# A conformer block with dilated attention on one core: the far statistics' read behind the next head's loads, and one filler step behind the last gate pair

## The chip, the core and the metric

The kernel runs on 1 core of one Trainium2 chip. The metric is the device time of one execution in microseconds, as the median of several runs; before the change it is 1699.01 us (three runs, 1698.5 to 1700.75 us).

## What is computed

One layer on 1024 tokens with 1024 channels, in float32. The attention is the part that the change touches:

```
z = rms_norm(x) @ w_in            # GLU input, q, k, v, gate logits
a = silu(rms_norm(causal_conv31(a_val * sigmoid(a_gate))));  y_a = a @ w_conv_out
for window, dilation in ((128, 1), (512, 4), (2048, 16)):
    o_g, lse_g = dilated_window_attention(q, k, v, slopes, window, dilation)
o = sum_g softmax_g(lse_g) * o_g;                            y_b = o @ w_attn_out
x = x + (sigmoid(g_a) * y_a + sigmoid(g_b) * y_b) @ w_out
x = x + (silu(u_gate) * u_val) @ w_down,  u = causal_conv3(rms_norm(x) @ w_up)
```

There are 16 heads of 64 dimensions. The three groups share one softmax over their logarithms of sums, so the kernel may weigh all keys of a query in one sum.

## The kernel before, in words

Every product of float32 matrices is made of three products of rounded parts (high x high, high x low, low x high; the halves are made by `split`, ScalarE the high part and VectorE the low one). The stages follow one another on PE: projections and GLU (to 180 us), q, k and v (to 457 us), the gate logits, five pairs of gate rows by a scheme of seven half-size products (to 579 us), then attention to 874 us, the output projections, and the feed-forward part to the end.

**Gate pairs.** The loop over `PAIRS` keeps a pair's sums in a PSUM tile `gx` (X and, for early pairs, a second half) and a bank `gy` (Y). The last pair, number 4, ends with three products of twelve matmuls each: X with `b12`, Y with `b22`, X with `form["t4"]`. ScalarE then copies X out (`c21`, L880). Scores of attention take tiles of the same pool `psA` of two tiles, so a score can need the tile that this copy frees.

**Attention.** The loop over `slots` has 8 slots for each head: places 0 to 3 score the first half of the queries, place 4 scores the far keys (distance of 512 and more in steps of 4, `score_far`), places 5 to 7 the second half. In each slot the code writes, in this order: the scores; filler steps of the side gemms (`fill(front)`; a step is three 128x512 matmuls of a gate or conv-out gemm, which keep PE at work while VectorE and ScalarE make powers); the transposes of the powers of a slot 12 earlier (`flip`) and the products with v of the slot before (`weigh`); the comparison and combination of statistics; the powers; statistics' transfers; `fill(behind)`. The engines ScalarE, VectorE, PE and GpSimd keep the written order inside this block. PE may still interleave two such blocks, here the gate pairs' block and attention's. SP, which issues nearly all transfers, is ordered by the framework's scheduler: an instruction is placed when the scheduler's model holds it ready. `tc.issue_after(x)` makes the instructions inside it follow `x` on the same engine, as an order and not as a wait.

**Statistics of a head.** A query of the second half has its near keys in one layout and its far keys in another (partition = position within a residue). Each has a minimum and a sum, in the tile `own` (near `own[:, 0]`, far `own[:, 1]`). Both layouts need the other's values in the tile `other`:

- `far_out` (L992): SP writes the far statistics to DRAM (`dstat`, 4 KB), two slots after the far scores.
- `near_to_far` (L989): four transfers of 1 KB move the near statistics from partition to partition into `other[:, 1]`, one slot after place 7.
- `far_to_near` (L995): SP reads `dstat` back in the other layout into `other[:, 0]`, in code five slots (`READ`) after the far scores, that is at place 1 of the next head. It must wait until the write has landed.
- `compare` (L999, L1000) on VectorE, nine slots after the far scores, needs all five transfers. `combine` (L1005 to L1008 and GpSimd's L975) comes one slot later and scales the powers.

**Loads.** At place 1 of head h the code calls `head(h + 1)`: q (512 KB, L155), two loads of k (512 KB each, L155), the mask (320 KB, L749), into tiles with two buffers. `values` loads v and vf (L155); `stage` loads weights for the side gemms (L93); `result` stores a head's half (L1072). SP's transfers use eight semaphores in turn, so that each also waits for the landing of the one eight before it.

Of the kernel before, what the change touches and what calls it, by code (L numbers as in the profile page):

```python
# [61 lines left out]
def block_kernel(ctx: ExitStack, tc: tile.TileContext, x, xT, x0, g2, pack, mask,  # L62
                 w_first, w_ch, w_qkv, w_co, w_ao, w_o, w_up, w_down, out):
    nc = tc.nc
    act, dve, pool, pe, sp = nc.scalar, nc.vector, nc.gpsimd, nc.tensor, nc.sync
# [240 lines left out]
    if True:  # L306
# [426 lines left out]
        def conv_result(c):  # L733
# [4 lines left out]
                           scale=pk[:, C_CG + c : C_CG + c + 1])  # L738
            act.dma_start(da[:, c, :], ordered)

        def head(h):
            hp, r, g8 = h // 2, (h % 2) * DH, h // 8
            q = p2.tile([P, T], F32R, tag="q", bufs=2, name=f"q_{h}")
            kk = p2.tile([P, 2, T], F32R, tag="kk", bufs=2, name=f"kk_{h}")
            m = p2.tile([P, 640], F32, tag="m", bufs=2, name=f"m_{h}")
            fetch(q, dq[g8].rearrange("p s c t -> (p s) c t")[2 * r : 2 * r + P, hp % 4, :])
            for s in range(2):
                fetch(kk[s:P:2], dk[g8][r : r + DH, :, hp % 4, :])
            sp.dma_start(m, mask[h])  # L749
            return q, kk[:, 0], kk[:, 1], m  # L750

        cover(COVER)
# [65 lines left out]
        with tc.manual_schedule(engines=hand):  # L818
            for n in range(2):
                xz[n] = gate_first(n, firsts[n])  # L820
                begun(n)
            load(1, 0)
            for n, (a, b) in enumerate(PAIRS):
                X = xz[n][:, 0:512]
                Y = bank_ps(f"gy_{n}")
                (sh, sl), (gh, gl) = pw[n]["s12"], pw[n]["s3"]
                inner = 0 < n < N - 1
                if n + 2 < N:
                    load(n + 2, 0)
                if n == 3:  # L830
                    p1_cm.__exit__(None, None, None)
                    p2_cm = tc.tile_pool(name="ph2", bufs=1, reuse_waits="tile")
                    p2 = p2_cm.__enter__()
                    pool2.append(p2)
                if n + 1 < N:
                    load(n + 1, 1)
                if n == 3:
                    tiles[0] = head(0)
                parts(n, "s4", "s4")
                if n == 0:  # L840
                    fourth()
                if inner:
                    parts(n + 1, 0, "v")
                product(X, sh[:, 4:8], sl[:, 4:8], *form["t2"], False)
                c12 = quarter(f"c12_{n}")
                act.activation(c12, X, AF.Copy)
                product(Y, sh[:, 0:4], sl[:, 0:4], *form["t1"], True)
                p5 = quarter(f"p5_{n}")
                act.activation(p5, Y, AF.Copy)
                if n == N - 1:  # L850
                    act.activation(warm, mhalf[:, 0:7], AF.Exp)
                if n == 0:
                    rs8 = conv_factors()
                if n == 2:
                    for c in (2, 3, 4, 5):
                        conv_result(c)
                product(X, gh[:, 0:4], gl[:, 0:4], *b12, False)
                if n == 1:
                    conv_spread(rs8)
                tt_(p5, X, p5, add)  # L860
                sp.dma_start(dgate[b][:, 512:1024], p5)
                if n + 1 < N:
                    sums(n + 1)
                if inner:
                    xz[n + 1] = big_ps(f"gx_{n + 1}")
                    for i in range(2):
                        product(xz[n + 1][:, i * 512 : i * 512 + 512], *(t[:, 4 * i : 4 * i + 4] for t in pw[n + 1]["v"]),
                                *left[i], True)
                    parts(n + 1, 2, "s12")
                    begun(n + 1)  # L870
                    for c in {1: (0, 1), 2: (6, 7)}.get(n, ()):
                        conv_result(c)
                else:
                    product(Y, *pw[n]["s4"], *b22, False)
                    tt_(c12, Y, c12, add)
                    if n + 1 < N:
                        parts(n + 1, 2, "s12")
                product(X, gh[:, 4:8], gl[:, 4:8], *form["t4"], False)
                c21 = quarter(f"c21_{n}")
                act.activation(c21, X, AF.Copy)  # L880
                sp.dma_start(dgate[b][:, 0:512], c21)
                if inner:
                    product(Y, *pw[n]["s4"], *b22, False)
                if n + 1 < N:
                    parts(n + 1, 1, "s3")
                if inner:
                    tt_(c12, Y, c12, add)
                sp.dma_start(dgate[a][:, 512:1024], c12)
# [7 lines left out]
    if True:  # L896
# [89 lines left out]

        def near_to_far(h):
            for i in range(4):
                sp.dma_start(other[h][32 * i : 32 * i + 32, 1], own[h][:, 0, i])  # L989

        def far_out(h):
            sp.dma_start(dstat[h % 2], own[h][:, 1])  # L992

        def far_to_near(h):
            sp.dma_start(other[h][:, 0], dstat[h % 2].rearrange("(i a) r s -> (a r) i s", i=4))  # L995

        def compare(h):
            f = ready2("both", [P, 2, 4], F32, 2, f"both_{h}")
# [75 lines left out]
        def fill(n):  # L1074
            for _ in range(n):
                next(gates, None)
# [33 lines left out]
        with tc.manual_schedule(engines={ENG.Activation, ENG.DVE, ENG.PE, ENG.Pool}):  # L1110
# [3 lines left out]
            for at in range(len(slots) + BACK + 1):  # L1114
                count[2] += 1
                cur = slots[at] if at < len(slots) else None
                front, behind = (FRONT[at % 8], BEHIND[at % 8] + (START[at] if at < BACK else 0)) if cur else TAIL
                new = []
                if cur is not None:
                    h, half, n = cur  # L1120
                    place = at % 8
                    if place == 4:
                        statistics(h)
                    if place == 5:
                        values(h)
                    if place == 1 and h + 1 < H:
                        tiles[h + 1] = head(h + 1)
                    new = score(h, tiles[h], SCORES[half][n])
                for unit in late:
                    share(*unit)  # L1130
                if len(pieces) > 2 and apart(at):
                    piece_high(2)
                fill(front)
                for n, soon in enumerate(COPIES):
                    if at == 0 and soon < 0 or cur is not None and (at - soon) % 8 == 0 and at - soon < len(slots):
                        by_residue((at - soon) // 8 if at else 0, n)
                flips = []
                if BACK <= at < len(slots) + BACK:
                    fh, fhalf, fn = slots[at - BACK]
                    if FLIPS[fhalf][fn]:  # L1140
                        flips.append(flip(fh, fhalf, FLIPS[fhalf][fn]))
                for w in pend:
                    done = weigh(*w) or done
                pend = flips
                late = []
                if done is not None:
                    result(*done)
                    done = None
                for ago, ready in ((BACK - 2, combine), (BACK - 3, compare)):
                    if 0 <= at - ago < len(slots) and slots[at - ago][1:] == (1, 0):  # L1150
                        ready(slots[at - ago][0])
                for unit in new:
                    powers(*unit)
                if cur is not None and half == 0:
                    late = new
                for ago, n0, send in ((2, 0, far_out), (1, 3, near_to_far), (READ, 0, far_to_near)):
                    if 0 <= at - ago < len(slots) and slots[at - ago][1:] == (1, n0):
                        send(slots[at - ago][0])
                if at == len(slots):
                    p2_cm.__exit__(None, None, None)  # L1160
                    hb2.append(ctx.enter_context(tc.tile_pool(name="hb2a", bufs=1, reuse_waits="tile")))
                    oT = [[hb2[0].tile([P, KT, 512], F32R, tag=f"hb{a}0", name=f"oT{a}0")] for a in range(2)]
                    heads = [o_fetch(0, k) for k in range(0, KT - 2, 2)]
                if at - len(slots) in (4, 5, 8, 9, 10, 11, 12):
                    o_step(heads)
                if at == len(slots) + BACK - 4:
                    heads.append(o_fetch(0, KT - 2))
                if apart(at):
                    piece_low()
                fill(behind)  # L1170
                if apart(at + 1):
                    piece_high(2)
            for _ in gates:
# [627 lines left out]
```

## Time and profile before

| | |
|---|---|
| median of 3 runs | 1699.01 us (1698.5 to 1700.75) |
| the profiled execution's own time | 1695.4 us |
| its span (first to last instruction) | 1693.6 us |
| granted TensorE clock | 1.0 over the whole span |
| busy PE, VectorE, ScalarE, GpSimd | 99%, 77%, 47%, 13% of the span |
| transfers, mean over the span | 177 GB/s |
| one head in the attention stage | some 17.5 us |

The profile is of one execution. Its page sums the busy time of each engine; the views used below are the table of waits (who waited for whom: total us, times, longest us), an engine's instructions in order of time (start, duration, engine, line, operation, tiles, and in brackets the idle time ahead and what ended it), the landing times of a line's transfers, and the row of digits that gives the busy tenths of the transfer engines in 40 slices. PE is a matmul, SPq an instruction of SP's queue. Heads are counted from 0; a head's row is told by its time.

### The profile page before, as it was taken

What the parts mean: (1) busy time and instruction counts of PE and PEld (TensorE: products, weight loads), DVE (VectorE), ACT (ScalarE), POOL (GpSimd) and SP (SyncE); (2) the same over time, 40 slices, a digit from 0 to 9 for tenths busy, and PEclk for the clock granted to TensorE, in tenths of its full rate; (3) what the DMA queues carried; (4) which work ended last, traced back from release to release, by engine and by line L of the source; (5) the groups of instructions that cost most, each with busy time, mean ns of one, the idle gap of its engine ahead of it and who ended that gap; (6) DMA issues with size and microseconds to landing.
All of it is one profiled execution on the core that took longest, in us unless ns stands there. A gap on an engine that the chain in (4) does not pass through costs nothing.

```text
span 1693.6 us, 22622 instructions
## 1 busy us (share of the span) xinstructions
PE 1681.4 (99%) x7939; PEld 1397.1 (82%) x7939; DVE 1303.1 (77%) x2114; ACT 787.9 (47%) x1351; POOL 224.3 (13%) x300
## 2 busy tenths in 40 slices
PE   9999999999999999999999999999999999999999
PEld 7888888888888888888888888888888888888887
DVE  6999999999876567767658654887777677789863
ACT  5411233233245478767646433544544455543431
POOL 0000132033000255555410000000000000000000
PEclk9999999999999999999999999999999999999999
DMA  9411145344555977886769594622222222499851
GB/s 375 153 50 50 50 137 162 125 137 137 175 178 195 320 226 238 261 243 201 221 214 333 187 335 147 227 99 76 75 90 85 87 75 87 145 366 322 287 172 50
DMA packets 187121, 300.24 MB, mean 177 GB/s; under 512 B 32256, under 2 KB 90240, under 8 KB 186496
## 3 DMA queue, kind: packets, MB, share of 16 engines
q1 hardware_dynamic: 185712, 294.48, 52.1%
q10 hardware_dynamic: 1296, 4.33, 0.6%
q8 instruction: 62, 1.02, 0.2%
q14 instruction: 51, 0.42, 0.1%
HBM read 214.74 MB, written 83.95 MB: 176 GB/s over the span
## 4 chain that ended last, share of the span: by engine, by line
PE 92%; DMA 3%; DVE 2%; ACT 1%; issue 1%; SPq 0%; POOL 0%; ACTq 0%; DVEq 0%
PE dx L1607 7%; PE xz L144 6%; PE xz L145 6%; PE xz L146 6%; PE dy L1607 5%; PE qkv L139 5%; PE qkv L137 5%; PE qkv L138 5%; PE y L145 2%; PE y L144 2%; PE y L146 2%; PE pp L1023 2%; PE wo L138 2%; PE wo L139 2%; PE wo L137 2%; PE o L1062 2%
## 5 line engine op out<-in xcount | busy, mean ns | idle before, releaser
L137 PE MATMUL qkv<-hi_qkv,hT 128*128 128x512 f32 x384 | 151.2, 395 | 0.0
L139 PE MATMUL qkv<-hi_qkv,hT 128*128 128x512 f32 x384 | 149.8, 391 | 0.0
L138 PE MATMUL qkv<-lo_qkv,hT 128*128 128x512 f32 x384 | 149.8, 391 | 0.0
L1510 DVE SCALAR_TENSOR_TENSOR u<-u,pk 128x1023 f32<-128x1023 f32 x88 | 112.1, 1275 | 1.2 <-ACT u L1508 0.9
L113 POOL TENSOR_TENSOR rs<-ss,mhalf 128x8 f32<-128x8 f32 x32 | 66.3, 2074 | 294.0 <-DVE ss L112 294.0
L1045 DVE TENSOR_TENSOR pl<-pp,ph 128x512 fp32r<-128x512 f32 (+1 forms) x95 | 58.7, 618 | 46.7 <-ACT ph L1044 46.5
L586 DVE SCALAR_TENSOR_TENSOR cacc<-csum,both,cacc 128x512 f32<-128x512 f32 x120 | 89.4, 745 | 0.3
L586 DVE SCALAR_TENSOR_TENSOR cacc<-apad,pk,cacc 128x512 f32<-128x512 f32 x120 | 88.2, 745 | 0.0
L89 DVE TENSOR_TENSOR lo_uv<-raw_uv,hi_uv 128x1024 fp32r<-128x1024 f32 x20 | 24.5, 1226 | 79.4 <-ACT hi_uv L88 79.4
L139 PEld LDWEIGHTS qkv<-hi_qkv,hT 128*128 128x128 f32 x384 | 72.1, 188 | 15.0
L586 DVE SCALAR_TENSOR_TENSOR codd<-apad,pk,codd 128x513 f32<-128x513 f32 x112 | 83.7, 748 | 0.7 <-ACT codd L579 0.7
L138 PEld LDWEIGHTS qkv<-lo_qkv,hT 128*128 128x128 f32 x384 | 72.2, 188 | 14.3
L137 PEld LDWEIGHTS qkv<-hi_qkv,hT 128*128 128x128 f32 x384 | 72.1, 188 | 14.2
L928 DVE CUSTOM_DVE_ANT_0 p<-s,m 128x512 f32<-128x512 f32 (+1 forms) x120 | 59.1, 502 | 17.2 <-POOL pf L975 6.3
L1044 ACT ACTIVATE ph<-pp 128x512 fp32r<-128x512 f32 (+1 forms) x95 | 51.5, 542 | 43.9 <-PE pp L1023 43.1
L144 PE MATMUL xz<-h2left,hi_uv 128*128 128x512 f32 x176 | 68.6, 390 | 0.0
L144 PE MATMUL xz<-blk_t,hi_s3g 128*128 128x512 f32 x176 | 68.6, 390 | 0.0
L146 PE MATMUL xz<-h2left,lo_uv 128*128 128x512 f32 x176 | 68.5, 389 | 0.0
L145 PE MATMUL xz<-h2left,hi_uv 128*128 128x512 f32 x176 | 68.5, 389 | 0.0
L145 PE MATMUL xz<-blk_t,hi_s3g 128*128 128x512 f32 x176 | 68.5, 389 | 0.0
L146 PE MATMUL xz<-blk_t,lo_s3g 128*128 128x512 f32 x176 | 68.5, 389 | 0.0
L1508 ACT ACTIVATE u<-u,pk 128x1024 f32<-128x1024 f32 x44 | 54.5, 1239 | 9.5 <-DVE u L1497 4.5
(479 smaller groups left out, 5056.5 us busy)
## 6 DMA issues: line engine op xcount, KB each, us to landing
wr<-w_down SPq DMA_DIRECT2D x45, 512.0 KB, 5.9
kk<-dk SPq DMA_DIRECT2D x32, 512.0 KB, 6.1
gr<-dff SPq DMA_DIRECT2D x62, 256.0 KB, 5.4
raw_qkv<-w_qkv SPq DMA_DIRECT2D x24, 512.0 KB, 4.9
dff<-u SPq DMA_DIRECT2D x22, 512.0 KB, 2.6
raw_uv<-w_up SPq DMA_DIRECT2D x21, 512.0 KB, 3.7
raw_ug<-w_up SPq DMA_DIRECT2D x20, 512.0 KB, 3.6
dv<-v SPq DMA_DIRECT2D x16, 512.0 KB, 2.8
```

The source lines that it names most:

```text
L113: pool.tensor_tensor(out=dst, in0=tmp, in1=mhalf[:, : tmp.shape[1]], op=ALU.pow)
L137: pe.matmul(ps, ah, hi[:, k % 2, :], start=(k == 0), stop=False)
L138: pe.matmul(ps, ah, lo[:, k % 2, :], start=False, stop=False)
L139: pe.matmul(ps, al, hi[:, k % 2, :], start=False, stop=(k == KT - 1))
L144: pe.matmul(o, wh[:, k, :], bh[:, k, :], start=(start and k == 0), stop=False, skip_group_check=not start)
L145: pe.matmul(o, wh[:, k, :], bl[:, k, :], start=False, stop=False, skip_group_check=not start)
L146: end = pe.matmul(o, wl[:, k, :], bh[:, k, :], start=False, stop=(k == 3), skip_group_check=not start)
L586: dve.scalar_tensor_tensor(out=out_, in0=src[:, i : i + size], scalar=w(i), in1=out_, op0=ALU.mult, op1=ALU.add)
L928: dve.tensor_tensor_reduce(out=pt, in0=s, in1=m, scale=-1.0, scalar=3e38, op0=ALU.add, op1=ALU.min, accum_out=nm)
L1045: dve.tensor_tensor(out=runs(pl[:, c]), in0=order(pp[:, c]), in1=runs(ph[:, c]).bitcast(F32), op=ALU.subtract)
L1510: dve.scalar_tensor_tensor(out=acc[:, d:], in0=src[:, : T - d], scalar=w(2 - d), in1=acc[:, d:], op0=ALU.mult, op1=ALU.add)
L1607: pe.matmul(banks[n][:, cols], a[:, c], b[:, d], start=(start and i == 0 and m == 0), stop=(stop and i == nf - 1 and m == 2), skip_group_c ...
```

## The change

Two edits. A list `queued` holds SP's last issue of interest: `near_to_far` puts its last transfer there, and `head` the mask's load. `far_to_near` is placed behind what `queued` holds. When it is called for head h, at place 1 of head h + 1, `head(h + 2)` has just been called, so the read follows the mask load of head h + 2; for heads 14 and 15 no load follows and it stands behind a near transfer. Second, the product of X with `form["t4"]` is kept as `paired` (after the loop: pair 4's), and in slot 0 the step of `fill(behind)` is placed behind its last matmul.

```
+        queued = []
...
-            sp.dma_start(m, mask[h])
+            queued[:] = [sp.dma_start(m, mask[h])]
...
-                product(X, gh[:, 4:8], gl[:, 4:8], *form["t4"], False)
+                paired = product(X, gh[:, 4:8], gl[:, 4:8], *form["t4"], False)
...
-                sp.dma_start(other[h][32 * i : 32 * i + 32, 1], own[h][:, 0, i])
+                queued[:] = [sp.dma_start(other[h][32 * i : 32 * i + 32, 1], own[h][:, 0, i])]
...
-            sp.dma_start(other[h][:, 0], dstat[h % 2].rearrange("(i a) r s -> (a r) i s", i=4))
+            with tc.issue_after(queued[0].ins):
+                sp.dma_start(other[h][:, 0], dstat[h % 2].rearrange("(i a) r s -> (a r) i s", i=4))
...
-                fill(behind)
+                with tc.issue_after(paired.ins) if not at else ExitStack():
+                    fill(behind)
```

On VectorE, ScalarE and GpSimd the order stays as it is. On SP the read moves in heads 1 to 13 behind the mask's load; in head 0 it stood there already; in heads 14 and 15 it moves behind one near transfer. SP in head 12 before (`own_7644` holds that head's statistics, `other_7645` receives; q, kk and m are head 14's, `dya` a store of a side gemm, `vf` values):

```order
L992 DMA dstat_139<-own_7644 128x8
L995 DMA other_7645<-dstat_139 128x4x2
L989 DMA other_7645<-own_7644 32x4x2 x2
L155 DMA q_7794<-dq_75 128x1024
L155 DMA kk_7795<-dk_77 64x2x1024
L1072 DMA do<-ot_0_7764 128x512
L989 DMA other_7645<-own_7644 32x4x2 x2
L155 DMA kk_7795<-dk_77 64x2x1024
L749 DMA m_7796<-mask 128x640
L249 DMA dya_104<-ya_0_7811 128x512
L155 DMA vf_7936<-dv_79 128x4x128
```

The same stretch of SP in the changed kernel, whose lines from L741 on are numbered two or three higher (L994 is the write, L991 a near transfer, L998 the read):

```order
L994 DMA dstat_139<-own_7644 128x8
L991 DMA other_7645<-own_7644 32x4x2 x2
L155 DMA q_7794<-dq_75 128x1024
L155 DMA kk_7795<-dk_77 64x2x1024
L1075 DMA do<-ot_0_7764 128x512
L991 DMA other_7645<-own_7644 32x4x2 x2
L155 DMA kk_7795<-dk_77 64x2x1024
L751 DMA m_7796<-mask 128x640
L249 DMA dya_104<-ya_0_7811 128x512
L998 DMA other_7645<-dstat_139 128x4x2
L155 DMA vf_7936<-dv_79 128x4x128
```

The read has gone from directly behind its write to behind ten other issues.

On PE the one difference is in slot 0 of head 0. Before, at the end of gate pair 4 (`gx_4554` is X, `gt_3354` and `gt_3355` the parts of `form["t4"]`, `s_31` the score of head 0's second unit, `gate_0` a filler step):

```order
L144 MATMUL gx_4554<-gt_3354,hi_s_4_4614 128x512
L145 MATMUL gx_4554<-gt_3355,hi_s_4_4614 128x512
L146 MATMUL gx_4554<-gt_3354,lo_s_4_4615 128x512
L924 MATMUL s_31_4741<-kk_4493,q_4492 128x384
L925 MATMUL s_31_4741<-kk_4493,q_4492 128x384
```

The same place in the changed kernel:

```order
L144 MATMUL gx_4554<-gt_3354,hi_s_4_4614 128x512
L145 MATMUL gx_4554<-gt_3355,hi_s_4_4614 128x512
L146 MATMUL gx_4554<-gt_3354,lo_s_4_4615 128x512
L120 MATMUL gate_0_4736<-hT_229,hi_gt_4722 128x512
L121 MATMUL gate_0_4736<-hT_230,hi_gt_4722 128x512
L122 MATMUL gate_0_4736<-hT_229,lo_gt_4723 128x512
L926 MATMUL s_31_4741<-kk_4493,q_4492 128x384
L927 MATMUL s_31_4741<-kk_4493,q_4492 128x384
```

Three matmuls now stand between the last matmul on X and the score; before, these three stood 36 matmuls earlier, between the score s_30 and the product of X with `b12`.

## The prediction

> **What bounds the kernel now.** The page's first table comes first, since it says which engine the end follows.
>
> ```profile
> PE 1681.4 (99%) x7939; PEld 1397.1 (82%) x7939; DVE 1303.1 (77%) x2114; ACT 787.9 (47%) x1351; POOL 224.3 (13%) x300
> ```
>
> TensorE is busy 1681.4 us of a span of 1693.6 us, so an edit that takes no product away can only win time in which PE stands idle: some 12 us in the whole kernel. The second view is the table of waits for PE alone, in the attention stage (560 to 880 us), where both edits act. The columns are the total in us, the number of waits and the longest.
>
> ```profile
> PE o L1062 <- DVE pl L1045: 5.3, 7, 1.7
> PE s L924 <- ACT c L880: 0.7, 1, 0.7
> PE s L924 <- DMA kk<-dk: 0.5, 1, 0.5
> PE o L1062 <- DVE pl_far L1045: 0.4, 1, 0.4
> PE s L924 <- issue: 0.2, 1, 0.2
> ```
>
> These sum to 7.1 us. That is the stock from which the change must draw. The third view is SP's own waits in 580:880, and behind it SP's instructions in order of time in head 12, the worst one.
>
> ```profile
> SPq L995 <- DMA dstat<-own: 68.7, 15, 5.4
> ```
>
> ```profile
> 795.74 0.38 SPq L992 DMA_DIRECT2D dstat<-own  x1
> 801.39 0.37 SPq L995 DMA_DIRECT2D other<-dstat  x1
> 801.85 1.26 SPq L989 DMA_DIRECT2D other<-own  x2
> 803.22 0.53 SPq L155 DMA_DIRECT2D q<-dq  x1
> ...
> 805.12 1.57 SPq L989 DMA_DIRECT2D other<-own  x2
> 806.74 0.64 SPq L155 DMA_DIRECT2D kk<-dk  x1
> 807.42 0.59 SPq L749 DMA_DIRECT2D m<-mask  x1
> 808.11 0.38 SPq L249 DMA_DIRECT2D dya<-ya  x1
> ```
>
> SP issues the write of the far statistics at 795.74 and then nothing until 801.39: the read back (L995) waits for that write to land, and the near statistics, the next q, k and mask stand behind it. Over 15 heads that is 68.7 us, 4.6 us a head. A stalled SP costs nothing by itself. What it delays shows on VectorE and then on PE:
>
> ```profile
> 811.29 0.17 DVE L999 TENSOR_TENSOR both<-own,other 128x8 f32<-128x8 f32 x1 [2.04 <-DMA kk<-dk]
> ```
>
> ```profile
> 813.26 0.39 PE L1062 MATMUL o<-pl,v 128*128 128x256 f32 x1 [1.71 <-DVE pl L1045]
> ```
>
> The comparison (L999) could have begun at 811.29 - 2.04 = 809.25. It needs the four transfers of near statistics and the far read. The read had been issued at 801.39; the second pair of near transfers, issued from 805.12 on, was late. (The releaser's name, kk, is that of another transfer counted by the same semaphores.) VectorE runs in order, so the next pl is late too, and PE loses 1.71 us.
>
> **Edit 1, the read behind the loads.** Nothing is added or removed; in heads 1 to 13 one 4 KB read moves behind q, kk, do and m in SP's order. In head 12 the near transfers would start at about 795.74 + 0.38 + 0.08 = 796.20 in place of 801.85, so everything behind moves up by 5.65 us: the mask to 801.77, the dya store to 802.46, and the read follows at about 802.92. By then the write is 7.2 us old, so the read waits no more. Behind it on SP stand the loads of the next values (vf, v) and the stores, which wait for PE and ScalarE as now. What PE gets back are the waits that follow a late load or a late comparison. Besides head 12's they are these, PE's first and VectorE's behind them:
>
> ```profile
> 760.60 0.47 PE L924 MATMUL s<-kk,q 128*128 128x512 f32 x1 [0.55 <-DMA kk<-dk]
> 764.34 0.33 PE L1062 MATMUL o<-pl_far,vf 128*128 128x128 f32 x1 [0.38 <-DVE pl_far L1045]
> 777.05 0.39 PE L1062 MATMUL o<-pl,v 128*128 128x256 f32 x1 [0.30 <-DVE pl L1045]
> 831.54 0.47 PE L924 MATMUL s<-kk,q 128*128 128x512 f32 x1 [0.22 <-issue]
> ```
>
> ```profile
> 762.99 0.69 DVE L928 CUSTOM_DVE_ANT_0 p<-s,m 128x512 f32<-128x512 f32 x1 [3.16 <-DMA m<-mask]
> 775.64 0.17 DVE L999 TENSOR_TENSOR both<-own,other 128x8 f32<-128x8 f32 x1 [1.19 <-DMA kk<-dk]
> ```
>
> At 760.60 the k load is late, at 764.34 the mask (3.16 us on VectorE), at 777.05 the comparison (1.19 us), and 831.54 is a first score that I put down to its k load as well. The sum is 1.71 + 0.55 + 0.38 + 0.30 + 0.22 = 3.16 us of idle PE. Matmuls start faster than they last, so an idle stretch costs more than its figure:
>
> ```profile
> 579.01 0.39 PE L145 MATMUL gx<-gt,hi_s 128*128 128x512 f32 x1
> 579.24 0.39 PE L146 MATMUL gx<-gt,lo_s 128*128 128x512 f32 x1
> 580.31 0.44 PE L924 MATMUL s<-kk,q 128*128 128x384 f32 x1 [0.69 <-ACT c L880]
> ```
>
> A matmul starts every 0.23 us and lasts 0.39, so each of the five stretches hides 0.16 more: 0.8, together 3.96 us. The Trainium skill (Perfetto Trace Analysis, Identifying the Most-Contended Engine) calls matmul busy time a bad measure of headroom because matmuls are pipelined. These rows agree: idle time alone would make the edit 3.2 us, the starts make it 4.0.
>
> From that I take 0.4 back. One kind of wait for pl owes nothing to SP, such as
>
> ```profile
> 664.69 0.39 PE L1062 MATMUL o<-pl,v 128*128 128x256 f32 x1 [0.38 <-DVE pl L1045]
> 731.58 0.50 PE L1062 MATMUL o<-pl,v 128*128 128x512 f32 x1 [1.07 <-DVE pl L1045]
> ```
>
> where VectorE is behind with side splits; with PE ahead of where it was, I expect one more of 0.38. So edit 1 is -3.6 us. Its bounds: above, 0, if the loads gain nothing; below, these pl waits vanish too, which with 5.3 + 0.4 + 0.5 + 0.2 = 6.4 us idle and 10 x 0.16 is -8.0 us at the very most. One of the seven (1.1 us) lies at the end of the stage behind other transfers, so I take -7.
>
> **Edit 2, the filler step.** Three 128x512 matmuls leave the place ahead of pair 4's last three products (twelve matmuls each) and stand between the last of them and the score s_31. At 580.31 that score waits 0.69 us for ScalarE's copy of the pair's bank (L880), since it takes that bank. The distance 579.24 to 580.31 is 1.07 us where 0.23 would do. Those three products start 0.7 us earlier, and so does the copy; the step's 3 x 0.23 = 0.69 us fill the time in which it runs. Gain -0.7 us, bounds 0 and -0.84. In front the step covered nothing: the product behind it needs the bank copied out by
>
> ```profile
> 566.97 0.60 ACT L846 ACTIVATE c<-gx 128x512 f32<-128x512 f32 x1
> ```
>
> which ends at 567.57, three microseconds ahead. The tie is an order on PE alone and adds no wait.
>
> **Sum.** The profiled execution took 1695.4 us, 1.8 more than its span. -3.6 - 0.7 = -4.3 makes 1691.1 there; the runs' median, 1699.01, lies 3.6 above that execution, and on it the forecast is 1694.7 us, -0.25%. About 0.2% (3.4 us) is what a measurement of this kernel tells from no change.
>
> **Rival 1: the comparison waits for the read instead.** This is the case that ends slower. Head 0 has the new order already, since its read stood behind the mask. The first rows are SP's and VectorE's there, the third L995's landings in all heads, the fourth the mask's.
>
> ```profile
> 595.14 0.58 SPq L749 DMA_DIRECT2D m<-mask  x1
> ...
> 596.26 0.41 SPq L995 DMA_DIRECT2D other<-dstat  x1
> ```
>
> ```profile
> 602.35 0.17 DVE L999 TENSOR_TENSOR both<-own,other 128x8 f32<-128x8 f32 x1 [0.80 <-DMA raw_a<-da]
> ```
>
> ```profile
> DMA to landing us min/median/max: 1.9/1.9/6.0
> ```
>
> ```profile
> DMA to landing us min/median/max: 5.7/6.3/9.7
> ```
>
> Alone the read lands in 1.9 us; behind the loads it took 6.0, and the comparison waited 0.80. In head 12 a read issued at 802.92 lands at 808.9 with 6.0 us, 0.35 ahead of the turn at 809.25; with the mask's worst, 9.7, at 812.6, 3.4 late. So the rival decides from 6.3 us on. At 2 us late, each comparison costs PE what head 12's 2.04 us did, 1.71: in 13 heads +22 us, less the 0.7 and less what loads alone give back (0.55 + 0.38 + 0.22 + 0.5 = 1.6): +20, 1719 us; half as late costs nearer 0.4 a head and ends at about +3. The Trainium skill (DMA: Bandwidth & Descriptors, Queues, rings and completion order) says that each DMA engine consumes a ring's descriptors in order, which speaks for it and against the edit; head 0's 6.0 against 1.9 agrees. Against the rival: head 12 is the tightest because SP was late there. Where it is on time the turn comes long after the write, as in head 1:
>
> ```profile
> 599.93 0.33 SPq L992 DMA_DIRECT2D dstat<-own  x1
> ```
>
> ```profile
> 618.44 0.16 DVE L999 TENSOR_TENSOR both<-own,other 128x8 f32<-128x8 f32 x1
> ```
>
> 18.5 us, where 7.2 + 6.0 = 13.2 are needed, and the edit returns SP to time. I give it 0.10.
>
> **Rival 2: the stall goes, the loads hardly move.** SP's transfers take eight semaphores in turn, so an issue also waits until the one eight before has landed, and loads of 6 us each behind one another keep it waiting. In 580:880 the profile has such waits:
>
> ```profile
> SPq L93 <- DMA kk<-dk: 5.6, 6, 1.9
> ```
>
> Then the comparison's wait in heads 10 and 12 is halved at best, about half of edit 1 is left (-1.8) and with edit 2 -2.5: 1696.5 us; if nothing of edit 1 is left, -0.7 and 1698.3 us. For it speaks that the transfer engines are full before and behind each stall; against it that they run dry in each stall, as the DMA row of 686 to 730 us shows (40 slices, tenths busy):
>
> ```profile
> DMA  9999999931378799999999982139789997999960
> ```
>
> There are two holes of some 3 us, one a head, which earlier loads would fill. Chance 0.33. That the change does not do what it says is not open: the order shows it.
>
> **How the numbers follow.** Forecast 0.57 at 1694.7; it spans 1691.3 (-7 and -0.7) to 1696.3, its upper part inside 0.2%. Rival 2 has 0.33, from 1696.3 to 1699.0, rival 1 0.10. The range takes the forecast's lower bound and all of rival 2: 1691.3 to 1699.0. Faster by over 0.2% means below 1695.6: most of the forecast, 0.53; within 0.2%: rival 2 and the rest, 0.37; slower 0.10.
>
> **What would show it.** Right: SP has no wait at L995; the mask's issue follows the write's by about 6 us in place of 11.7; L999 waits in no head but the first; PE has no wait of 1.71 for pl nor any for kk, and s_31 starts within 0.4 us of the matmul ahead of it. Wrong: L999 waits 1 us or more in most heads (rival 1), or the k loads land as late as now (rival 2), or new waits of PE for pl of 0.4 us and more in many heads, which would show that VectorE and not SP sets the slots.

## The result, and the profile after

The changed kernel takes 1690.05 us in the median of six runs (1689.05 to 1691.13), the kernel before 1697.34 us in six beside them (1693.84 to 1700.75). The ratio is 0.9958, 95% interval 0.9943 to 0.9972: 7.3 us faster by the medians. The forecast was 1694.7 with a range of 1691.3 to 1699.0, so the direction was right and the gain larger than the range allowed.

The two profiled executions differ by less: 1691.13 us after (span 1689.3) against 1695.4 (span 1693.6), 4.3 us. That is the forecast's sum to the tenth; it is luck in part, as the sums further down show.

PE's waits in 556:876, the table that gave the stock of 7.1 us before, now have one row (total in us, number, longest):

```profile
PE o L1065 <- DVE pl L1048: 4.3, 5, 2.1
```

The waits for ScalarE's copy, for a kk load and for pl_far are gone, and so are two of the waits for pl. SP's waits in 580:880 were led by 68.7 us for the write of the far statistics. Now they read

```profile
SPq L991 <- ACT p L974: 25.1, 32, 1.6
SPq L155 <- PE o L1065: 23.1, 9, 4.4
...
SPq L998 <- DMA dstat<-own: 2.0, 2, 1.7
```

SP now waits for what the engines have yet to make; 2.0 us for the write are left, in the last heads, which have no next mask to queue behind. Here is head 12 on SP in order of time, to be held against the rows from 795.74 on in the prediction:

```profile
785.77 0.92 SPq L1075 DMA_DIRECT2D do<-ot  x1
787.40 0.33 SPq L994 DMA_DIRECT2D dstat<-own  x1
789.33 2.40 SPq L991 DMA_DIRECT2D other<-own  x2
...
793.74 1.52 SPq L991 DMA_DIRECT2D other<-own  x2
...
795.98 0.58 SPq L751 DMA_DIRECT2D m<-mask  x1
...
797.24 0.43 SPq L998 DMA_DIRECT2D other<-dstat  x1
```

The first thing to see isn't the missing hole but the times at the left: the write (L994) goes out at 787.40 where it went out at 795.74. Of these 8.3 us, 2.8 are the kernel's own gain up to there (ScalarE's copy below, at 785.15 in place of 787.94); the rest is that SP was late. The store of the outputs (do<-ot) shows it directly, since that copy releases it. Before, the copy and its store (the 22nd of 32 each) were

```profile
787.94 0.60 ACT L1070 ACTIVATE ot<-o 128x512 f32<-128x512 f32 x1 [0.19 <-PE o L1062]
```

```profile
792.85 2.80 SPq L1072 DMA_DIRECT2D do<-ot  x1
```

and after, the copy of the store at 785.77 was

```profile
785.15 0.60 ACT L1073 ACTIVATE ot<-o 128x512 f32<-128x512 f32 x1
```

From the copy's end to the end of the store's issue it was 795.65 - 788.54 = 7.1 us before, and it is 786.69 - 785.75 = 0.9 us now. Counted in the same way, k-th copy to k-th store, the sixteen stores of 11 to 26 stood 7.3 us behind on average before, and 1.0 after. SP was a whole 7 us behind the engines through heads 5 to 12, and the change brought it back to time. The sum of SP's waits doesn't show this: all that the view lists for 580:880 comes to 173 us before and 174 after. The near statistics ride on that: the comparison (L999 before, L1002 now) waits in no head but the first.

```profile
L1002 DVE TENSOR_TENSOR both<-own,other x15: 156/156/168, 602.2 to 839.2; 128x8 f32<-128x8 f32 x15
...
  DMA raw_a<-da: 1.0, 1
```

Before, the same view had 0.8 us in head 0 and 5.2 in five others:

```profile
  DMA kk<-dk: 4.4, 4
  DMA raw_a<-da: 0.8, 1
  DMA other<-own: 0.8, 1
```

Edit 2 shows as forecast: the score s_31 starts 0.40 us after the matmul ahead of it (it was 1.07), with the filler step (its last matmul is the first row) in the place of the wait.

```profile
579.57 0.39 PE L122 MATMUL gate<-hT,lo_gt 128*128 128x512 f32 x1
579.97 0.45 PE L926 MATMUL s<-kk,q 128*128 128x384 f32 x1
```

Last, the end of the stage. The first row is before, the second after:

```profile
875.36 0.44 PE L1062 MATMUL o<-pl,v 128*128 128x384 f32 x1 [1.11 <-DVE pl L1045]
```

```profile
870.73 0.44 PE L1065 MATMUL o<-pl,v 128*128 128x384 f32 x1 [2.07 <-DVE pl L1048]
```

PE arrives there at 868.66 in place of 874.25, 5.6 us earlier, and leaves 4.6 us earlier. A microsecond is given back in one wait. VectorE's rows say what for:

```profile
868.98 1.23 DVE L1101 TENSOR_TENSOR raw_o<-raw_o,oT 128x1024 f32<-128x1024 f32 x1 [1.98 <-DMA oT<-do]
870.13 0.55 DVE L1048 TENSOR_TENSOR pl<-pp,ph 128x384 fp32r<-128x384 f32 x1
```

An add of the output projection waits for a load of the last heads' outputs, and the pl that PE needs stands behind it in VectorE's order. The wait has a sequel: from 871.54 on the granted TensorE clock is 0.5 for 3.4 us (0.91 over 860:880, where before has 1.00), and there a 128x512 matmul starts every 0.43 us in place of 0.23.

### The profile page after: what moved, and what is told of

The parts are those of the page before. It is cut to its first block, busy times and chain, and to the rows that moved or that the text cites. A ratio compares the mean times of both kernels' runs of the same rounds, so it can differ in the third digit from the quotient of the medians.

```text
span 1689.3 us, 22626 instructions
## 1 busy us (share of the span) xinstructions
PE 1680.0 (99%) x7939; PEld 1398.5 (83%) x7939; DVE 1301.9 (77%) x2114; ACT 786.4 (47%) x1351; POOL 224.5 (13%) x300
## 4 chain that ended last, share of the span: by engine, by line
PE 97%; DVE 1%; DMA 1%; ACT 1%; issue 1%; POOL 0%; SPq 0%; ACTq 0%; DVEq 0%
PE dx L1611 7%; PE xz L144 6%; PE xz L145 6%; PE xz L146 6%; PE dy L1611 5%; PE qkv L137 5%; PE qkv L139 5%; PE qkv L138 5%; PE y L145 2%; PE y L146 2%; PE y L144 2%; PE pp L1026 2%; PE wo L138 2%; PE wo L139 2%; PE yb L122 2%; PE yb L120 2%
```

## The experiments

The first theory (theory 1 below) is that the prediction's stalls are the right ones, but of a size that differs from execution to execution. The rival (theory 2) is that the executions differ for another reason, say the clock, so that edit 1 is worth its 3.6 us and the rest of 7.3 is the choice of executions. The times:

| run | median us (runs) | before beside it (runs) | ratio, 95% interval |
|---|---|---|---|
| c1_before | 1697.15 (11) | 1697.49 (21) | 1.0000, 0.9991 to 1.0010 |
| e1_read_only | 1690.58 (5) | 1697.49 (21) | 0.9964, 0.9952 to 0.9977 |
| e2_step_only | 1694.62 (11) | 1697.49 (21) | 0.9984, 0.9975 to 0.9993 |
| c2_after | 1690.80 (5) | 1697.49 (21) | 0.9963, 0.9951 to 0.9976 |
| f1_late_add | 1690.38 (5) | 1696.71 (21) | 0.9959, 0.9947 to 0.9972 |
| f3_compare_late | 1701.01 (11) | 1696.71 (21) | 1.0025, 1.0016 to 1.0034 |
| f5_second_wait | 1711.49 (4) | 1696.71 (21) | 1.0082, 1.0066 to 1.0097 |
| h1_loads_ahead | 1697.46 (10) | 1696.71 (21) | 1.0003, 0.9994 to 1.0012 |
| g1_behind_piece | 1692.86 (5) | 1696.80 (21) | 0.9968, 0.9956 to 0.9981 |
| e3_start_later | 1697.16 (11) | 1696.80 (21) | 1.0001, 0.9992 to 1.0010 |
| e4_step_again | 1696.10 (11) | 1696.80 (21) | 0.9995, 0.9986 to 1.0004 |
| c3_before | 1696.47 (1) | 1696.80 (21) | a single run |

The ratio is taken over all runs, so it isn't quite that of the two medians. Where a difference is given in us below, it is the ratio's.

### Both kernels again: c1_before, c3_before, c2_after

No edit.

> The kernel before, unchanged, to see how much one execution of it differs from the next. Theory 1 (the prediction's stalls, but of a size that differs from execution to execution: SP's wait for the statistics' write makes the loads and the comparison late by an amount that depends on the transfers, and the profiled execution of 1695.4 us was one with small stalls): its profiled execution has another sum of PE's idle time than the 9.03 us of the first profile, and the difference in time from 1695.4 us follows that sum (an execution of 1698 us has about 11.5 us idle), with the difference in heads 6 to 14 (560 to 880 us) and at the comparison's wait for the far read. Theory 2 (the executions differ for reasons that have nothing to do with these stalls, say the clock or the start): PE's idle time in 560 to 880 us stays within 0.5 us of the first profile's whatever the time.

> One more look at the kernel before, for another profiled execution. Theory 1: its time follows the comparison's waits and PE's idle time: at 1697 to 1699 us the comparison's waits in heads 6 to 13 are 2 to 4 us more in sum than the 5.5 us of the first profile; at 1695.5 us they are the same within 1 us.

> The changed kernel again. Its profiled execution had PE idle for 2.07 us at 870 us, where before had 1.11 us at 875 us, and a granted clock of 0.94 in 870 to 900 us. If that gap belongs to the changed order, it is there again within 0.3 us; if it is chance, it is 1.1 us or less and the execution ends nearer to 1689.8 us. Median 1690 us, spread under 2.5 us; -7.3 us against before by the medians so far, -4.3 us if the kernel before is as quick in this run as its profiled execution was.

The kernel before has now 81 runs: median 1696.8 us, 1692.9 to 1700.8. The changed kernel has 11: median 1690.4, 1689.05 to 1691.63. So the difference is 6.4 us, and the kernel before spreads over 7.9 us where the changed one spreads over 2.6. The base on which the forecast stood, the 1699.01 us of three runs, was thus 2.2 us too high; the medians of 21 runs in the table say the same.

The profiled executions of before took 1695.4, 1695.18 and 1696.47 us, with PE idle in all for 9.03, 9.51 and 10.14 us. The third is 1.1 us above the first in both figures, as theory 1 has it, and its PE waits in 556:886 show where:

```profile
PE o L1062 <- DVE pl L1045: 5.0, 7, 1.5
PE s L924 <- DMA kk<-dk: 2.3, 1, 2.3
PE s L924 <- ACT c L880: 0.7, 1, 0.7
```

One wait for a k load grew from 0.55 to 2.3 us. But the comparison's waits in heads 6 to 13 sum to 3.5 us there and not to more than the first profile's 5.2, so "the comparison's waits set an execution's time" is too narrow: a late SP shows now at the comparison, now at a k load. The second is against the theory by 0.7 us (0.5 us more idle, 0.2 less time). No execution of 1698 us or more was caught with a profile.

The clock of theory 2 does take part, though not on its own account. From shortly before the end of c3's wait of 2.3 us the granted clock is 0.5 for 3.4 us (763.8 to 767.2); in the other two profiles of before it is 1.0 throughout the stage. A mean clock is on record for 74 more executions of before: 41 at 1.000 took 1696.4 us in the mean, 27 at 0.999 took 1697.4, and six at 0.998 or 0.997 took 1699.2. So the slow executions tend to have lost clock as well as time in waits. It is a part of the spread only, since those at 1.000 alone lie between 1692.9 and 1699.7 us. Ten of the changed kernel's 11 runs are at 1.000.

c2_after has the wait at 870 us again, at 1.14 us in place of 2.07 and with no drop of the clock behind it, so the wait belongs to the changed order and its size varies by a microsecond.

### One edit at a time: e1_read_only, e2_step_only, e4_step_again, e3_start_later

e1 is the diff without these lines:

```
-                paired = product(X, gh[:, 4:8], gl[:, 4:8], *form["t4"], False)
+                product(X, gh[:, 4:8], gl[:, 4:8], *form["t4"], False)
...
-                with tc.issue_after(paired.ins) if not at else ExitStack():
-                    fill(behind)
+                fill(behind)
```

e2 and e4 are the kernel before with those lines alone.

> Edit 1 alone (the read queued behind the mask load; the first slot's filler step as before). The prediction's sum gives -3.6 us for it, -4.3 for both. Theory 1: it carries nearly all of the difference of the medians, -6 to -7 us, and takes the spread of the executions away with it (before spreads over some 7 us, this one over 2 or less). Theory 2: about -3.6 us, and it spreads as before does. The comparison waits for nothing but in the first head.

> Edit 2 alone (the first slot's filler step behind pair 4's last matmul; the read as before). The prediction gives -0.7 us, bounds 0 and -0.84. Both theories: -0.7 us, which the spread of the kernel before may hide (it keeps that spread by theory 1). A rival, that edit 2 is worth more than its own 0.7 us because all later work moves against the transfers: -2 us or more.

> Edit 2 alone a second time, with new executions of before beside it. If -2.9 us was mostly chance of the executions that were drawn, it is nearer to -0.7 us; if it is the kernel's, it is -2 to -3.5 us again. Its profile should again have the comparison waiting in five or more of the heads 6 to 13.

e1 is 6.1 us faster than before (interval 3.9 to 8.1), and its five runs lie within 1.5 us: edit 1 carries the whole gain and takes the spread with it, which is theory 1's case. Its PE waits in 556:886 are the changed kernel's, and the 0.7 us that edit 2 takes away:

```profile
PE o L1065 <- DVE pl L1048: 3.2, 5, 1.1
PE s L926 <- ACT c L882: 0.7, 1, 0.7
```

e2 measured -2.7 us at first and -0.8 the second time (interval -2.4 to +0.7). Both intervals hold -1.5, and both traces show the 0.7 us at 580 and no other systematic gain; in both the comparison waits in heads 0, 6, 7, 10, 11 and 12, as before. Against e1, the full change is 0.2 us slower by the medians of the same batch, with 5 runs each. So edit 2's 0.7 us is seen in the trace at its place, and the time can tell it neither from nothing nor from a microsecond and a half.

Was the first -2.7 a matter of phase, of the later work falling otherwise against the transfers?

```
+                for _ in range(4 if h == 0 and i == 2 else 0):
+                    pe.matmul(s[:, c], q[:, i * P : (i + 1) * P], kh[:, ks], start=True, stop=True)
                 scored(s[:, c], q[:, i * P : (i + 1) * P], kh[:, ks], kl[:, ks])
```

> The kernel before with four more products of 128x384 on PE in the second slot of the first head (0.17 us each, overwritten by what follows them): all of the later work starts about 0.7 us later, as edit 2 alone starts it 0.7 us earlier. Edit 2 alone measured -2.9 us (interval -4.2 to -1.2), and 0 on top of edit 1. If a shift is passed on as it is, this is +0.7 us (0 to +1.2). If a shift against the transfers changes the comparison's waits (so that edit 2 alone got 2 us by a favourable phase), it is outside of that, to either side.

It came to +0.2 us (interval -1.4 to +1.7), which holds +0.7. Nothing points to a phase.

### More of the suspected wait: f5_second_wait

```
             sp.dma_start(other[h][:, 0], dstat[h % 2].rearrange("(i a) r s -> (a r) i s", i=4))
+            sp.dma_start(dtwice[h % 2], other[h][:, 0])
```

> The kernel before with one more small write in each head, whose source is the far read: SP waits a second time, until the read has landed, behind the first or second piece of the near statistics (about 1.0 us of waiting, and 0.4 to 0.65 us to issue). Nothing needs what it writes; it holds back the last pieces and the next head's loads by about 1.5 us more. Theory 1: the comparison's waits grow by up to 1.5 us in each of heads 6 to 13, and PE pays most of it: +5 to +12 us. Against it (SP has slack enough, and the difference of edit 1 has another source): 0 to +1 us.

SP's first two waits in 580:886, and PE's in 556:886 (two of 0.7 us follow):

```profile
SPq L996 <- DMA dstat<-own: 69.1, 15, 5.8
SPq L997 <- DMA other<-dstat: 15.4, 13, 4.1
```

```profile
PE o L1064 <- DVE pl L1047: 11.5, 7, 3.9
PE s L925 <- issue: 2.7, 2, 1.6
```

It is 13.9 us slower (11.2 to 16.5) for 15.4 us of additional waiting and sixteen more issues of 0.34 us, about 21 us of SP in all; more than was expected. The waits are only a part of it. The two profiled executions are 17.0 us apart; PE's waits in 556:886 grow by 8.5 us, from 7.1 to 15.6, and at the end of three of them the granted clock falls to 0.5, for 3.4 us at 657.5, 6.8 at 715.5 and 6.8 at 773.6, which can cost up to another 8.5. Here is the second of the three (behind the window: its length, busy time and number for PE, PEld, VectorE, ScalarE and GpSimd, then the granted clock, and the transfers' share and GB/s):

```profile
700.00:715.50 15.50, 11.99 (x72) 10.21 (x70) 9.26 (x32) 9.80 (x30) 3.08 (x5) 1.00 0.79 239
715.50:722.40 6.90, 6.48 (x19) 5.50 (x20) 3.43 (x14) 3.51 (x10) 5.93 (x11) 0.51 0.94 323
```

Before, SP's whole 68.7 us cost some 6. So the price of SP's time isn't a fixed share of it: it is small as long as there is slack, and beyond that each of the 21 us here cost 0.4 us of waiting, and 0.7 to 0.8 with the clock. The kernel before stood just beyond that point. The largest wait names the way, the comparison of head 6 waiting for the near statistics:

```profile
714.50 0.17 DVE L1001 TENSOR_TENSOR both<-own,other 128x8 f32<-128x8 f32 x1 [4.81 <-DMA other<-own]
715.92 0.58 PE L1064 MATMUL o<-pl,v 128*128 128x256 f32 x1 [3.92 <-DVE pl L1047]
```

### Less of it: g1_behind_piece

The read goes behind the first ready piece of the near statistics, ahead of everything else (edit 2 left out):

```
-            queued[:] = [sp.dma_start(m, mask[h])]
+            sp.dma_start(m, mask[h])
```

> Edit 1 with another place for the read: behind the first piece of the near statistics that is ready, ahead of the other three pieces and of all of the next head's loads (edit 2 left out). SP waits for the write's landing 2 to 3.5 us in each head in place of 4.6, but until the same moment, so that the last pieces and the loads come only 0.4 to 0.65 us earlier than before. Theory 1 (what counts is when SP gets past the landing, since the last pieces, which the comparison waits for, stand behind it): -1 us against before (0 to -2), the comparison's waits still there, the spread too. If what counts is how long SP waits, about half of edit 1's gain: -3 us or more.

```profile
790.37 0.39 SPq L994 DMA_DIRECT2D dstat<-own  x1
790.86 0.59 SPq L991 DMA_DIRECT2D other<-own  x1
795.60 0.37 SPq L998 DMA_DIRECT2D other<-dstat  x1
796.06 0.58 SPq L991 DMA_DIRECT2D other<-own  x1
```

```profile
SPq L998 <- DMA dstat<-own: 51.3, 15, 5.3
```

```profile
  DMA raw_a<-da: 1.1, 1
  DMA other<-own: 0.4, 1
```

The rows are SP's in head 12, SP's wait in 580:880 and the comparison's waits. Theory 1 as I had put it falls here. SP still waits 51.3 of 68.7 us, and the last three pieces still stand behind the landing, yet the comparison's waits are down to 0.4 us outside of head 0 and the time is 5.4 us below before (3.2 to 7.5), most of edit 1's gain. Nor is the gain in proportion to the wait, as the other reading had it: a quarter of the wait went. It is the edge that f5 shows from the other side. One piece less behind the wait moves SP's lag from 7.3 to 5.7 us (stores 11 to 26 again), and there the pieces land ahead of the comparison's turn, by 0.2 to 1.8 us in heads 6 to 13 (head 7 alone waits, for 0.4). How much of this is the lag and how much the piece that went ahead, this run doesn't tell apart.

### The comparison's wait alone: f3_compare_late

```
-                for ago, ready in ((BACK - 2, combine), (BACK - 3, compare)):
+                for ago, ready in ((BACK - 2, compare), (BACK - 2, combine)):
```

> The kernel before, with the comparison of a head's statistics one slot later (in the slot of the combination, ahead of it), the read and the loads where they were. It takes away the comparison's waits, and leaves SP's. Theory 1 (the gain of edit 1 is mostly that the comparison on DVE no longer waits for pieces of the near statistics, which SP issues behind its wait): -3 to -6 us against before, the PE waits behind the comparison gone, the spread smaller. Theory 2 (it is mostly the late q, kk and mask loads): under -1.5 us, and the spread of the kernel before stays.

It is 4.2 us slower, which neither theory had. The waits did go: SP waits as before, the comparison never, and PE's table in 556:886 has no k load and less pl.

```profile
SPq L995 <- DMA dstat<-own: 70.1, 15, 6.1
```

```profile
PE o L1062 <- DVE pl L1045: 3.0, 6, 1.1
PE s L924 <- ACT c L880: 0.7, 1, 0.7
```

What it costs instead is in the transposes of the far units, which need what the combination has scaled on GpSimd. The first row is this kernel in head 12, the second before:

```profile
800.09 1.37 PE L1023 MATMUL pp_far<-ident,pf 128*128 128x128 f32 x4
```

```profile
795.80 1.07 PE L1023 MATMUL pp_far<-ident,pf 128*128 128x128 f32 x4
```

The four start as GpSimd finishes each, and not one right behind the other: 0.3 us in this head. Over the 16 heads the distance from the first of the four to the last sums to 14.4 us where it was 6.9. The 7.5 us more are above the loss, so the waits that went did give some 3 us back. That is an estimate and no weighing of edit 1, since the slower heads also give the loads more time. What the run tells better: with SP as late as ever (6.8 us for the stores 11 to 26) and the comparison free of waiting, 11 runs lie within 1.8 us (1700.13 to 1701.92), all at a clock of 1.000, where the 21 of before beside them spread over 5.9. That points to the comparison as the way by which the spread of the kernel before comes; the longer time for the loads is not excluded as a part of it.

### Rival 1 on purpose: h1_loads_ahead

```
+            spare = ready2("spare", [P, 2, T], F32R, 1, f"spare_{h}")
             with tc.issue_after(queued[0].ins):
+                for s in range(2):
+                    fetch(spare[:, s], dq[h // 8].rearrange("p s c t -> (p s) c t")[s * P : s * P + P, h // 2 % 4, :])
                 sp.dma_start(other[h][:, 0], dstat[h % 2].rearrange("(i a) r s -> (a r) i s", i=4))
```

> The changed kernel with two more loads of 128x1024 in each head between the mask load and the far read (their data isn't used). By the landings of head 12 in the changed kernel (a kk half of 0.5 MB lands 2.1 us behind the transfer ahead of it) the read lands 4 to 5 us later, where it had 1.7 to 4.8 us to spare in heads 6 to 13. If rival 1's mechanism is real, with its deciding point where this slack ends, the comparison waits for the far read in most of these heads by 0 to 3 us, and PE pays: +5 to +15 us against the changed kernel. If the read is not held back by the loads ahead of it, 0 to +1 us.

The read's landings in all heads, first in the changed kernel and then here, and head 7's read and comparison here:

```profile
DMA to landing us min/median/max: 1.9/5.5/7.5
```

```profile
DMA to landing us min/median/max: 4.2/7.6/8.7
```

```profile
719.26 1.04 SPq L1001 DMA_DIRECT2D other<-dstat  x1
```

```profile
728.19 0.17 DVE L1005 TENSOR_TENSOR both<-own,other 128x8 f32<-128x8 f32 x1 [1.68 <-DMA dya<-ya]
```

That read landed 8.7 us after its issue, at 727.97, 0.2 ahead of the comparison, so it is the read that was waited for. In eight heads the comparison waits 11.0 us in all, 4.0 of them in head 0; PE waits for no k load. The time is 6.8 us above the changed kernel's (ratios 1.0003 and 0.9963), all of the gain gone, and the ten runs spread over 5.1 us again. The rival was real. It decides somewhat later than the prediction put it (6.3 us): head 7's turn here would have come 728.19 - 1.68 - 719.26 = 7.3 us behind the read's issue. The change stays on the good side of it: in head 12 its read lands at 797.24 + 5.8 = 803.0, 3.0 us ahead of the comparison at 806.05. The Trainium skill (DMA: Bandwidth & Descriptors, Queues, rings and completion order) has descriptors consumed in ring order on each engine; the landings of 1.9 us alone, 5.5 behind a head's loads and 7.6 behind two loads more agree with it.

### The wait that gives gain back: f1_late_add

```
-                if at - len(slots) in (4, 5, 8, 9, 10, 11, 12):
+                if at - len(slots) in (4, 5, 8, 10, 11, 12):
```

> The changed kernel with one thing moved: in the tail the fourth sum of the output projection (the add that waits for the load of the last heads' far half) goes one slot later, behind the low part of a flip that TensorE waits for. In the three profiled executions with the read behind the mask PE is idle for 2.07, 0.99 and 1.14 us there (870 us), each time until that load has landed at 868.9 to 869.7 us. If this wait is what bounds the tail after the change, it goes and the time falls by 1 us (0.5 to 1.5) against the changed kernel's 1690.4 us; if the output projection's first product at 897 us then waits instead (0.54 and 0.83 us in two of the three), half of it or all comes back: 0.

The wait for pl at 870 us is gone, and the median is 1690.38 against 1690.4 for the changed kernel: nothing. Two other waits stand in its place, ahead of products of the output projection: 0.41 us at 870.80 for ScalarE's hi_ao, and 0.94 at 896.24 for VectorE's gg.

No version here beats the changed kernel by more than the runs can tell.

## Why the prediction was right in direction and wrong in size

**What bounds the kernel** held. PE is busy 1680.0 of 1689.3 us, and the gain came out of PE's waits and late starts in 560:880.

**Edit 1, the waits listed** held. Of the five PE waits put down to the read, all are gone, and the pl waits put down to VectorE (664.69 and 731.58) are still there, at 664.47 and 730.68. The 0.4 us taken back for one more of them did not come at that place; a microsecond was given back at 870 us, in the one wait that the bound had set aside as lying behind other transfers.

**Edit 1, its size** was too small even against the profiled execution. PE reaches the wait at 870 us 5.6 us earlier. It had lost 0.3 us at the start, in a wait that no edit touches (the same matmul of L427 starts at 7.72 before, and at 8.02 after, behind 0.47 us of waiting for ScalarE).

Edit 2 gave 0.7, so edit 1 had given 5.6 + 0.3 - 0.7 = 5.2 us by there, where the sum had 4.0 for the five waits and 3.6 with the 0.4 taken back. Set matmul against matmul, the five places give back 0.71 + 0.54 + 0.47 + 1.88 + 0.39 = 4.0 us, just the sum's term. The 1.2 us more stand in no wait of the table: they come in steps of up to 0.15 us, mostly at products with v that started a little late before, behind one that still counted as busy. That the two profiled executions met the sum of 4.3 is misses that cancel, and luck: 1.6 us too little for edit 1, against 0.3 lost at the start, 1.0 given back at 870 us and 0.3 behind it (1.4 lost at the halved clock, 1.1 regained further on).

**The step that failed** is the last of the sum: "the runs' median, 1699.01, lies 3.6 above that execution, and on it the forecast is 1694.7". It carried the gain of one execution to the median as if the distance were the same in both kernels. It isn't. On 81 runs the kernel before lies 1.4 us above its first profiled execution (1696.8 against 1695.4); the changed kernel lies 0.7 below its own (1690.4 against 1691.13). 4.3 + 1.4 + 0.7 is the 6.4 us measured. Of the rest of the miss 2.2 us are the base, a median of three runs. What the runs showed in place of a constant: SP was 7 us late, at the edge of the comparison's slack, where a little more or less in the transfers is passed on (f5: 13.9 us for 21 of SP's time, up to half of it by way of the clock; g1: most of the gain for a quarter of the wait; f3: little spread once the comparison doesn't wait). An execution of before loses now more, now less at that edge, in waits and, where one is long, in clock behind it; the change takes that loss away. The typical loss is inferred from the spread, the medians and the mean clocks; an execution at the upper end was not caught with a profile, and which transfers vary stays open.

**The picture of SP** was the wrong one for the same reason. The prediction took a hole of 5.65 us out of head 12 and moved what stands behind it by as much. The mask was to follow the write by 6 us; it follows by 8.6 (795.98 - 787.40, it was 11.7), because SP, on time now, waits for ScalarE between the pieces. The gain lies in the write's own time.

**Edit 2** was right in the trace (s_31 after 0.40 us, 0.67 less than before), and too small for the measured times to tell.

**Rival 1** was rightly held back, by the argument that was given: once SP is on time the comparison's turn comes long after the write. h1 shows that it was no idle worry. **Rival 2** is refuted: the loads moved with SP (in head 12 the second k load lands at 801.29 in place of 813.47).

## What to carry to other kernels

Look for how late the issuing engine is, and not only for how long it waits: the distance from a copy's end to the issue of its store is read off two rows. A queue that runs late but within everyone's slack costs little, and beyond the slack each further microsecond costs a good part of one; here the kernel on that edge showed it by runs that spread. When a change takes such a kernel off the edge, expect the spread to go too: don't add the profiled execution's distance from the median to the forecast as if it stayed, and take that median from more than three runs. When a run gets slower by more than its waits, look at the granted clock behind the long ones.

## What the hardware showed unasked

In the kernel before, the issue of one output store often takes long: in 690:815 its duration in ns was, min, median and max, first before and then after,

```profile
L1072 SPq DMA_DIRECT2D do<-ot x14: 399/549/3231, 698.5 to 812.2; - x14
```

```profile
L1075 SPq DMA_DIRECT2D do<-ot x15: 328/539/1454, 691.3 to 810.1; - x15
```

All of before's above 1.5 us (eight in the stage, up to 3.2 us) came when five to seven of SP's earlier transfers had not landed yet, and the copy that the store needs had ended 0.3 to 6.5 us earlier. So an SP that is late, and issues its loads and stores in a burst, also issued more slowly. Not every issue behind as many was slow, and no run here tells what SP waits for inside it.

In these traces the granted clock falls to 0.5, for 3.4 or 6.8 us, at the end of every single PE wait of 1.87 to 2.80 us in the attention stage and its tail (g1, after, c3 and f5) and of 3.92 us (f5), and at two pairs of waits close together (1.45 and 1.00 us in e3, 1.79 and 0.71 in f5). It doesn't at a single one of 1.71 us or less, nor at h1's wait of 3.00 us at 606 us, so the length alone doesn't decide. So a wait can cost more than its own length: 1.4 us more, for the 2.07 us of the changed kernel's profile.
